# All eleven gate and up blocks as seven products, the first two units interleaved, the first unit's weights split beside the output projection

## The chip, the cores and the metric

The kernel runs on one core of a Trainium2 chip. The metric is the device time of one execution in microseconds (us). One execution was also profiled; its trace gives every instruction's start and duration on the engines: PE is TensorE (matmul), PEld its weight loads, DVE VectorE, ACT ScalarE, POOL GpSimd. SP only issues transfers (DMAs) here.

## What is computed

One layer: three token mixers read a normalised input, their gated sum goes through an output projection and is added to x; then a normalised feed-forward part follows, which is where the change lies. Its sizes: 512 tokens, width 1024, `w_gate` and `w_up` 1024 x 2816, `w_down` 2816 x 1024.

```python
    merged = ...
    x = x + merged @ w_out[layer]

    h2 = rms_norm(x, g_ffn[layer])
    x = x + (jax.nn.silu(h2 @ w_gate[layer]) * (h2 @ w_up[layer])) @ w_down[layer]
```

## The kernel before, in words

**Precision.** Each operand of a matmul is split into a high part (a rounded copy, made by ScalarE) and a low part (what is left, a subtraction on VectorE). A product then takes three passes: high by high, high by low, low by high (`PASSES`).

**Order.** The program is written out by hand: each engine executes its own instructions in the order in which the code emits them, and waits at an instruction until its inputs are there and its output buffer is free. `mm` (L211) emits a matmul and calls `tick` (L196) after each 13 or so of 256 columns; a tick emits half a weight piece's split (`split_next`, L145) and what `later` (L231) has put off for so many ticks. SBUF tiles come from one ring of 47 slots (`slot`, L56), PSUM banks from two rings, three "m" and five "a" (`bank`, L78). SP executes its DMA issues in order too; one that waits holds those behind it.

**Output projection.** `out_group(t, c, W)` (L927) computes token tile t (of four) by 256 columns c (of four): 24 matmuls; VectorE then adds the bank to the residual (tile `x`, L930), ScalarE squares it and sums the squares (`sq`, L932). Columns 0 and 1 are done for all t, then columns 2 and 3 for t = 0, 1, 2, 3 in turn, each followed by `norm2(t)` (L953): the sum of squares, its root (ACT `ra`, `ry`; DVE `rv`, `ra`, `rr`), the normalised row tile `h` (L958), and a DMA of the residual to DRAM (`x_d`, L959), which SP issues when the last `x` of this t is there. After t = 2, `turn2(0)` (L961) transposes the tokens of t = 0 and 1 (16 matmuls against the identity) and evacuates them, split.

**Gate and up.** 2816 columns are eleven blocks of 256. Block 0 is computed plainly: `plain` (L1125, called in the loops below L1132), eight groups of 24 matmuls, with `turn2(1)` after the second group. The other ten blocks are *units*. A unit multiplies a 2 x 2 block matrix of weights by one of activations with seven products instead of eight (M1 to M7, of 24 matmuls each; `product`, L1061), from sums of quarters. `load_unit` (L1005) issues ten DMAs on SP, in this order: S1, S3, A11, A12, A22, each a gate half and an up half of 256 KB (tiles `wq`, L1010), and four adding DMAs on POOL, into S1 and S3. `sums` (L1020) makes S2 and S4 on VectorE (`ws`), `split_op` (L1025) makes the high part `wh` and the low part `wl` of one left operand, 128 x 1024 (L1029, L1030). The right operands are B11, B21, B22 (quarters of the transposed activations) and four sums T1 to T4, split once (`xh`, `xl`). `after` (L1082) evacuates the products, `glu` and its two helpers make silu(gate) x up, split, as tile `gT`. Unit 0 is loaded when the plain block begins; each product carries a list of hooks (`todo`) that are emitted between its matmuls: the evacuation of the product before, the split for the product after next, the loads of the next unit.

**Down.** `down` (L1204) multiplies `gT` by `w_down`, adds the residual and writes out.

Of the kernel before, what the change touches and what calls it, by code (L numbers as in the profile page):

```python
# [42 lines left out]
def hybrid_layer(ctx, tc, rope, x, mem, g_mix, w_in, b_forget, g_q_moba, g_k_moba, g_q_fox,  # L43
# [80 lines left out]
    plan_cols(w_gate, D, DFF, 0, 256)  # L124
    plan_cols(w_up, D, DFF, 0, 256)
# [808 lines left out]
    for c in range(2):  # L934
        W = take(2)
        for t in range(NT):
            out_group(t, c, W)
    W2, W3 = take(2), take(2)
    h2 = {}


    Xf, X = {}, {}
    for kh in range(2):
        for th in range(2):
            Xf[kh, th] = slot("xf")
            X[kh, th] = slot("xh", F32R), slot("xl", F32R)

    def quarter(t):
        return t[:, :1024].rearrange("p (k t) -> p k t", k=4)

    x1_d = dram.tile([NT, P, D], F32, name="x1_d")

    def norm2(t):  # L953
        s1 = sm("s1", 1, 4)
        dve.tensor_reduce(s1, ss2[:, t, :], axis=AX.X, op=OP.add)
        r = rsqrt(s1, 1.0 / D, 1)
        h2[t] = slot("h2")
        dve.tensor_scalar(h2[t][:, :D], x1[t][:, :D], r, None, op0=OP.mult)  # L958
        nc.sync.dma_start(x1_d[t], x1[t][:, :D])  # L959

    def turn2(u):  # L961
        for b4 in range(4):
            tb = bank("a")
            for k2 in range(2):
                k = 2 * b4 + k2
                for t2 in range(2):
                    o = k2 * 256 + t2 * P
                    pe.transpose(tb[:, o:o + P], h2[2 * u + t2][:, k * P:(k + 1) * P], ident)
            for k2 in range(2):
                k = 2 * b4 + k2  # L970
                hi, lo = (quarter(a)[:, k % 4, :] for a in X[k // 4, u])
                evac_split(hi, lo, tb[:, k2 * 256:(k2 + 1) * 256], gcol[:, GFFN + k:GFFN + k + 1])
            c = (2 * b4) % 4 * 256
            pool.tensor_tensor(Xf[b4 // 2, u][:, c:c + 512], f32(X[b4 // 2, u][0][:, c:c + 512]),
                               f32(X[b4 // 2, u][1][:, c:c + 512]), op=OP.add)
# [29 lines left out]
    def load_unit(u):  # L1005
        f0 = 256 * (u + 1)

        def quarter_of(e, t, kh, fh, **how):
            for g, w in enumerate((w_gate, w_up)):
                e.dma_start(  # L1010
                    t[:, g * 512:(g + 1) * 512].rearrange("p (k c) -> p k c", k=4),
                    dsrc(w, kh * 512 * DFF + f0 + fh * P, [[DFF, P], [P * DFF, 4], [1, P]]), **how)

        for name, kh, fh in (("S1", 0, 1), ("S3", 0, 1), ("A11", 0, 0), ("A12", 1, 0), ("A22", 1, 1)):
            t = L[u, name] = slot("wq")
            quarter_of(nc.sync, t, kh, fh)
        quarter_of(nc.gpsimd, L[u, "S1"], 1, 1, accum_op=OP.add)
        quarter_of(nc.gpsimd, L[u, "S3"], 0, 0, accum_op=OP.add)
# [6 lines left out]
    def split_op(u, m):  # L1025

        r = L[u, LEFT[m]]
        hi, lo = slot("wh", F32R), slot("wl", F32R)
        act.activation(full(hi), full(r), AF.Copy)  # L1029
        dve.tensor_tensor(full(lo), full(r), f32(full(hi)), op=OP.subtract)  # L1030
        H[u, m] = full(hi), full(lo)

    def right_sum(name, a, b, op, e):
        t = slot("xt")
        e.tensor_tensor(full(t), full(a), full(b), op=op)
        return t
# [24 lines left out]
    def product(u, m, hooks):  # L1061

        ps = banks[u, m] = bank(TAG[m])
        w = [a.rearrange("p (g k c) -> p g k c", g=2, k=4) for a in H.pop((u, m))]
        r = [quarter(a) for a in B[RIGHT[m]]]
        n = 0
        hooks = deque(hooks)
        for g in range(2):
            for k in range(4):
                for a, b in PASSES:  # L1070
                    pe.matmul(ps[:, g * 256:(g + 1) * 256], w[a][:, g, k, :], r[b][:, k, :],  # L1071
                              start=n % 12 == 0, stop=n % 12 == 11)
# [9 lines left out]
    def after(u, m):  # L1082

        if m == "M1":
# [28 lines left out]
    def glu_end(u, j):  # L1113
# [4 lines left out]
        gT[2 * (u + 1) + j] = (o[:, :512], o[:, 512:1024])  # L1118


    Wg, Wu = take(2), take(2)
    pace["ahead"] = 0
    ps4 = [bank("m"), bank("m"), bank("m"), bank("a")]

    def plain(W, f, ps, th):  # L1125
        for k in range(KD):
            for a, b in PASSES:
                mm(ps[:, th * 256:(th + 1) * 256], W[k // 4][a][:, k % 4, f * P:(f + 1) * P],
                   quarter(X[k // 4, th][b])[:, k % 4, :], 256,
                   (k == 0 and (a, b) == PASSES[0]), (k == KD - 1 and (a, b) == PASSES[-1]))  # L1130

    load_unit(0)  # L1132
    for half in range(2):
        for n, (W, f) in enumerate(((Wg, 0), (Wg, 1), (Wu, 0), (Wu, 1))):
            plain(W, f, ps4[n], half)
            if half == 0 and n == 1:
                turn2(1)
                for j, fn in enumerate(right_t()):
                    later(3 + j, fn)
            if half == 0 and n == 3:  # L1140
                for j, name in enumerate(("S2", "S4")):
                    later(3 + j, lambda name=name: sums(0, name))
                later(5, lambda: split_op(0, "M1"))
                later(6, lambda: split_op(0, "M2"))
    sl = slot("silu")
    for f in range(2):
        act.activation(sl[:, f * 512:(f + 1) * 512], ps4[f], AF.Silu)
    for f in range(2):
        s = sl[:, f * 512:(f + 1) * 512]
        dve.tensor_tensor(s, s, ps4[2 + f], op=OP.mult)  # L1150
        o = slot("gT", F32R)
        evac_split(o[:, :512], o[:, 512:1024], s)
        gT[f] = (o[:, :512], o[:, 512:1024])
    run_due()
    run_pend()
    while deferred:
        run_due()
        run_pend()
# [104 lines left out]
```

## Time and profile before

| | us |
|---|---|
| median of 3 runs (896.21 to 897.88) | 897.0 |
| the profiled execution | 897.43 |
| its span, first to last instruction | 895.6 |
| TensorE busy in it | 875.7 |
| VectorE busy | 566.1 |
| ScalarE busy | 448.8 |
| GpSimd busy | 202.8 |

A row of the timeline has the start in us from the span's start, the duration, engine, line of the kernel, operation, tiles written and read, shape, how many follow each other, and in brackets how long the engine was idle before it and what ended that. A row of a stage table has the stretch, its length, then for each engine the busy time and its instructions, then the granted TensorE clock (1.00 is full speed), the share of time in which the DMA engines were busy, and GB/s. Buffer numbers are left out of names there, so `x1` and `h2` of the code appear as `x` and `h`. A matmul of 256 columns shows about 0.28 us because matmuls overlap; their starts lie some 0.118 us apart.

### The profile page before, as it was taken

Reading aid. Unit: us, or ns where it says so; the run is one execution under the profiler, and the core shown is the slowest. Engines: PE = TensorE matmul, PEld = TensorE weight load, DVE = VectorE, ACT = ScalarE, POOL = GpSimd, SP = SyncE. Lnnn points to the kernel's source line nnn. Section 1 sums busy time; section 2 is a strip of 40 time slices with the busy share of each in tenths; the row PEclk is TensorE's granted clock in tenths of the full one; section 3 lists DMA queues with packets and bytes.
Section 4 is the critical chain, followed back from the end, with each engine's and each line's share of the span. In section 5 each row is a group of like instructions: output and inputs, shape, how many; then the busy total and the mean of one; then the engine's idle time right before and its main releaser. Section 6 shows DMA issues by size and latency. Waiting matters only on the chain.

```text
span 895.6 us, 15494 instructions
## 1 busy us (share of the span) xinstructions
PE 875.7 (98%) x5942; PEld 806.7 (90%) x5942; DVE 566.1 (63%) x1138; ACT 448.8 (50%) x942; POOL 202.8 (23%) x292
## 2 busy tenths in 40 slices
PE   6999999999999999999999999799999999999998
PEld 6999988998899899888888999699999999888886
DVE  4955764666566867787445367888888889842001
ACT  7755764665557557665333444544445445532000
POOL 3222421151212533533000017532222220000000
PEclk9999999999999999999999999799999999999999
DMA  9920332143313512523335019989986886851001
GB/s 309 285 70 25 97 93 71 49 122 92 95 49 112 149 48 70 167 71 119 117 121 186 1 72 196 251 164 179 175 166 120 184 163 144 303 194 48 1 35 59
DMA packets 128361, 111.25 MB, mean 124 GB/s; under 512 B 5072, under 2 KB 119816, under 8 KB 128288
## 3 DMA queue, kind: packets, MB, share of 16 engines
q1 hardware_dynamic: 104320, 93.37, 35.1%
q0 software_dynamic: 22784, 14.78, 11.7%
q10 hardware_dynamic: 1184, 2.12, 0.8%
q8 instruction: 47, 0.77, 0.4%
q14 instruction: 26, 0.21, 0.1%
HBM read 101.85 MB, written 4.21 MB: 118 GB/s over the span
## 4 chain that ended last, share of the span: by engine, by line
PE 86%; DVE 4%; ACT 3%; DMA 2%; POOL 2%; issue 1%; SPq 1%; ACTq 0%; POOLq 0%; DVEq 0%
PE ps_m L215 47%; PE ps_a L1071 13%; PE ps_m L1071 9%; PE ps_a L215 8%; PE ps_a L721 2%; PE ps_a L659 2%; PE ps_a L710 2%; DMA x_t<-in_x_dram 1%; DVE kT L479 1%; PE ps_a L462 1%; DVE w_lo L159 1%; ACT kT L475 1%; DMA wq<-in_w_gate_dram 1%; ACT w_hi L158 1%; PE ps_a L627 0%
## 5 line engine op out<-in xcount | busy, mean ns | idle before, releaser
L159 DVE TENSOR_TENSOR w_lo<-w_raw,w_hi 128x512 fp32r<-128x512 f32 (+1 forms) x212 | 146.0, 721 | 74.5 <-ACT w_hi L158 60.2
L215 PE MATMUL ps_m<-w_hi,hT 128*128 128x256 f32 (+1 forms) x896 | 168.2, 285 | 0.0
L215 PEld LDWEIGHTS ps_m<-w_hi,hT 128*128 128x128 f32 x896 | 139.4, 189 | 0.3
L158 ACT ACTIVATE w_hi<-w_raw 128x512 fp32r<-128x512 f32 (+1 forms) x212 | 123.9, 621 | 28.4 <-PE ps_m L215 19.0
L215 PE MATMUL ps_m<-w_lo,hT 128*128 128x256 f32 (+1 forms) x448 | 127.4, 284 | 0.5 <-DVE w_lo L159 0.5
L215 PE MATMUL ps_m<-hT,w_hi 128*128 128x512 f32 x384 | 123.2, 397 | 0.0
L1071 PE MATMUL ps_a<-xh,wl 128*128 128x256 f32 x320 | 91.2, 285 | 3.9 <-DVE wl L1030 3.9
L1071 PE MATMUL ps_a<-xh,wh 128*128 128x256 f32 x320 | 91.2, 285 | 2.6 <-ACT wh L1029 2.6
L1071 PE MATMUL ps_a<-xl,wh 128*128 128x256 f32 x320 | 91.1, 285 | 0.0
L215 PEld LDWEIGHTS ps_m<-w_lo,hT 128*128 128x128 f32 x448 | 84.5, 189 | 0.9 <-DVE w_lo L159 0.7
L215 PEld LDWEIGHTS ps_m<-hT,w_hi 128*128 128x128 f32 x384 | 71.0, 188 | 14.1
L692 POOL TENSOR_SCALAR p_t<-p_t,rc 128x128 f32<-128x128 f32 (+1 forms) x64 | 40.6, 635 | 171.5 <-DVE rc L691 142.7
L215 PE MATMUL ps_m<-hT,w_lo 128*128 128x512 f32 x192 | 76.5, 398 | 0.0
L215 PE MATMUL ps_a<-w_hi,gT 128*128 128x512 f32 x220 | 71.1, 392 | 0.0
L1071 PE MATMUL ps_m<-xl,wh 128*128 128x256 f32 x240 | 67.5, 281 | 0.0
L1071 PE MATMUL ps_m<-xh,wl 128*128 128x256 f32 x240 | 67.4, 281 | 0.0
L1071 PE MATMUL ps_m<-xh,wh 128*128 128x256 f32 x240 | 67.3, 280 | 0.0
L1071 PEld LDWEIGHTS ps_a<-xh,wl 128*128 128x128 f32 x320 | 61.6, 192 | 4.2 <-DVE wl L1030 4.2
L1071 PEld LDWEIGHTS ps_a<-xh,wh 128*128 128x128 f32 x320 | 61.7, 193 | 2.8 <-ACT wh L1029 2.8
L1030 DVE TENSOR_TENSOR wl<-wq,wh 128x1024 fp32r<-128x1024 f32 x50 | 60.8, 1218 | 2.0 <-ACT wh L1029 2.0
L215 PE MATMUL ps_m<-yT,w_hi 128*128 128x512 f32 x192 | 61.9, 397 | 0.0
L1071 PEld LDWEIGHTS ps_a<-xl,wh 128*128 128x128 f32 x320 | 61.7, 193 | 0.0
(221 smaller groups left out, 1969.0 us busy)
## 6 DMA issues: line engine op xcount, KB each, us to landing
w_raw<-in_w_in_dram SPq DMA_DIRECT2D x50, 512.0 KB, 3.8
wq<-in_w_gate_dram SPq DMA_DIRECT2D x50, 256.0 KB, 5.4
wq<-in_w_up_dram SPq DMA_DIRECT2D x50, 256.0 KB, 6.6
w_raw<-in_w_down_dram SPq DMA_DIRECT2D x22, 512.0 KB, 4.5
wq<-in_w_gate_dram POOLq DMA_DIRECT2D x20, 256.0 KB, 9.3
wq<-in_w_up_dram POOLq DMA_DIRECT2D x20, 256.0 KB, 10.4
w_raw<-in_w_mem_kv_dram SPq DMA_DIRECT2D x8, 512.0 KB, 9.7
kT<-kT POOLq DMA_DIRECT2D x16, 256.0 KB, 4.1
```

Source lines behind the costliest of these rows:

```text
L158: act.activation(hi[:, c], r[:, c], AF.Copy)
L159: pend.append(lambda: dve.tensor_tensor(lo[:, c], r[:, c], f32(hi[:, c]), op=OP.subtract))
L215: pe.matmul(ps, lhsT, rhs, start=start, stop=stop)
L462: pe.transpose(tb[:, tt * P:(tt + 1) * P], raw[:, tt * 256 + blk * P:tt * 256 + (blk + 1) * P], ident)
L475: act.activation(hi[r], tb[r], AF.Copy, scale=g[r])
L479: dve.scalar_tensor_tensor(lo[q if gc in (GQM, GQF) else r], tb[r], g[r], f32(hi[r]), op0=OP.mult, op1=OP.subtract)
L659: pe.matmul(ps[:, :n], Q[p][:, s * 512 + i * P:s * 512 + (i + 1) * P], K[p][s][:, b * 512:b * 512 + n], start=b == 0, stop=b == 1)
L692: pool.tensor_scalar(pt[:, :nk], pt[:, :nk], rc, 1.0, op0=OP.mult, op1=OP.mult)
L710: pe.transpose(tb[:, j * P:(j + 1) * P], pt[:, j * P:(j + 1) * P], ident)
L721: pe.matmul(yb[:, :256], V[p][:, j, 2 * s:2 * s + 2, :], PT[b][:, j, :], start=(j == 0 and b == 0), stop=(j == nj - 1 and b == 1))
L1030: dve.tensor_tensor(full(lo), full(r), f32(full(hi)), op=OP.subtract)
L1071: pe.matmul(ps[:, g * 256:(g + 1) * 256], w[a][:, g, k, :], r[b][:, k, :], start=n % 12 == 0, stop=n % 12 == 11)
```

## The change

The plain block is gone; all eleven blocks are units (`NU` from 10 to 11). Unit 0 is loaded before the output projection, and its seven splits and two sums are emitted at every second tick from column 1 of the projection on. The first two units' products are interleaved (`FIRST`). Units 2 to 10 follow in the old order with the old hooks. `turn2` now takes one quarter (kh, th): it evacuates unsplit (`xf`, alternately by ScalarE and VectorE), and `right_split` splits from there, B11 and B21 in two halves during t = 3, B22 and the sums T1 to T4 within the first products. What GpSimd added before VectorE now does. For units 0 and 1 M3 is evacuated ahead of M5 and M6, by a copy.

```diff
-    plan_cols(w_gate, D, DFF, 0, 256)
-    plan_cols(w_up, D, DFF, 0, 256)
...
+    FIRST = ((0, "M1"), (0, "M2"), (1, "M1"), (1, "M2"), (0, "M3"), (1, "M3"), (0, "M5"), (0, "M6"),
+             (1, "M5"), (1, "M6"), (0, "M7"), (1, "M7"), (0, "M4"), (1, "M4"))
...
+    Ws = take(2)
+    load_unit(0)
+    for c in range(2):
+        if c:
+            Ws = take(2)
+            for j, fn in enumerate((
+                    lambda: split_op(0, "M1"), lambda: sums(0, "S2"), lambda: split_op(0, "M2"),
+                    lambda: sums(0, "S4"), lambda: split_op(0, "M5"), lambda: split_op(0, "M3"),
+                    lambda: split_op(0, "M6"), lambda: split_op(0, "M7"), lambda: split_op(0, "M4"))):
+                later(2 + 2 * j, fn)
+        for t in range(NT):
+            out_group(t, c, Ws)
...
     for t in range(NT):
         out_group(t, 2, W2)
         out_group(t, 3, W3)
         norm2(t)
         if t == 2:
-            turn2(0)
+            for kh, name in ((0, "B11"), (1, "B21")):
+                turn2(kh, 0)
+                right_split(name, Xf[kh, 0], 2)
...
     use_table("silu_and_others")
+    load_unit(1)
...
-    load_unit(0)
-    for half in range(2):
-        for n, (W, f) in enumerate(((Wg, 0), (Wg, 1), (Wu, 0), (Wu, 1))):
-            plain(W, f, ps4[n], half)
...
-    order = [(u, m) for u in range(NU) for m in ORDER]
+    order = list(FIRST) + [(u, m) for u in range(2, NU) for m in ORDER]
...
+    todo[0] += [lambda: split_op(1, "M1")]
+    todo[1] += [lambda: split_op(1, "M2")]
+    todo[2] += [lambda: turn2(1, 1), lambda: turn2(0, 1), lambda: right_split("B22", Xf[1, 1]),
+                lambda: right_sum("T1", Xf[0, 0], Xf[0, 1], OP.subtract),
+                lambda: sums(1, "S2")]
+    todo[3] += [lambda: right_split("T1", T["T1"]), lambda: sums(1, "S4")]
+    todo[4] += [lambda: split_op(1, "M3"),
+                lambda: right_sum("T2", Xf[1, 1], T["T1"], OP.add),
+                lambda: right_split("N2", T["T2"], 1, -1.0)]
```

The products and their left operands are M1: A11, M2: A12, M3: S4, M4: A22, M5: S1, M6: S2, M7: S3.

**VectorE, token tile t = 1 of columns 2 and 3.** Before, from the normalised tile of t = 0 to that of t = 1:

```order
L958 TENSOR_SCALAR h_6382<-x_6008,rr 128x1024
L930 TENSOR_TENSOR x_6010<-ps_m,x_6010 128x256 x2
L955 TENSOR_REDUCE s_6441<-ss_6016 128x1
L267 TENSOR_SCALAR rv<-s_6441 128x1
L275 TENSOR_TENSOR ra<-ry 128x1
L276 SCALAR_TENSOR_TENSOR ra<-ra,rv 128x1
L277 SCALAR_TENSOR_TENSOR rr<-ra,ry 128x1
L958 TENSOR_SCALAR h_6453<-x_6010,rr 128x1024
```

The same place in the changed kernel (its lines are two to 42 off):

```order
L1000 TENSOR_SCALAR h_6385<-x_6008,rr 128x1024
L987 TENSOR_TENSOR wl<-ws,wh 128x1024
L928 TENSOR_TENSOR x_6010<-ps_m,x_6010 128x256
L987 TENSOR_TENSOR wl<-ws,wh 128x1024
L928 TENSOR_TENSOR x_6010<-ps_m,x_6010 128x256
L997 TENSOR_REDUCE s_6452<-ss_6016 128x1
```

One low part of unit 0 now stands ahead of each of the two residual adds; each needs its `wh`, which ScalarE makes behind the square of the `x` above it. The rows from the reduction on are the same.

**SP, from the last weights of the projection to the loads behind it** (`x1_d` is the residual in DRAM, `wq` a quarter of unit weights). Before:

```order
L141 DMA w_raw_6287<-in_w_up_dram 128x4x256
L959 DMA x1_d_6301<-x1_6008 128x1024
L959 DMA x1_d_6301<-x1_6010 128x1024
L959 DMA x1_d_6301<-x1_6012 128x1024
L959 DMA x1_d_6301<-x1_6014 128x1024
L1010 DMA wq_6655<-in_w_gate_dram 128x4x128
L1010 DMA wq_6655<-in_w_up_dram 128x4x128
```

Now:

```order
L963 DMA wq_6030<-in_w_up_dram 128x4x128
L139 DMA w_raw_6072<-in_w_out_dram 128x4x256
L139 DMA w_raw_6110<-in_w_out_dram 128x4x256
L1001 DMA x1_d_6017<-x1_6008 128x1024
L1001 DMA x1_d_6017<-x1_6010 128x1024
L1001 DMA x1_d_6017<-x1_6012 128x1024
L1001 DMA x1_d_6017<-x1_6014 128x1024
L963 DMA wq_6660<-in_w_gate_dram 128x4x128
L963 DMA wq_6660<-in_w_up_dram 128x4x128
L963 DMA wq_6663<-in_w_gate_dram 128x4x128
L963 DMA wq_6663<-in_w_up_dram 128x4x128
L963 DMA wq_6666<-in_w_gate_dram 128x4x128
```

Unit 0's ten loads have moved ahead of the projection's last two pieces; the first loads behind the four residuals are now those of unit 1. `wq_6666` is A11 of unit 1, the operand of the third product.

**ScalarE, from the loading of the silu table on**, where the products begin. Before:

```order
L63 ACT_TABLE_LOAD
L158 ACTIVATE w_hi<-w_raw 128x512 x4
L242 ACTIVATE xh<-ps_a,gcol 128x256 x8
L1040 ACTIVATE xh<-xt 128x1024 x4
L1029 ACTIVATE wh<-wq 128x1024 x2
```

Now:

```order
L63 ACT_TABLE_LOAD
L986 ACTIVATE wh<-wq 128x1024
L1099 ACTIVATE zs<-ps_a 128x512
L986 ACTIVATE wh<-wq 128x1024
L1017 ACTIVATE xf<-ps_a,gcol 128x256 x4
L1025 ACTIVATE xh<-xf 128x1024
L1099 ACTIVATE zs<-ps_a 128x512
L1025 ACTIVATE xh<-xt 128x1024
L986 ACTIVATE wh<-ws 128x1024
```

The high parts of A11 and A12 of unit 1 (the first and second `wh`) now stand ahead of the evacuations `xf` that B22 and T1 to T4 are made from; the last row is the high part of S4 of unit 1.

More of the change, by code (lines that the diff above doesn't have):

```diff
@@ L932, in out_group @@
         act.activation(sq, xs, AF.Square, accum_out=ss2[:, t, c:c + 1])
[L934 to L946, printed above, removed]
+    gT = {}
+    RIGHT = {"M1": "B11", "M2": "B21", "M3": "B22", "M4": "T4", "M5": "T1", "M6": "N2", "M7": "T3"}
@@ L948, in quarter, with full, load_quarters, quarter_of @@
+    def full(t):
+        return t[:, :1024]
     def quarter(t):
         return t[:, :1024].rearrange("p (k t) -> p k t", k=4)
+    PLACE = {"S1": (0, 1), "S3": (0, 1), "A11": (0, 0), "A12": (1, 0), "A22": (1, 1)}
+    def load_quarters(u, names):
+        f0 = 256 * u
+        def quarter_of(e, t, kh, fh, **how):
+            for g, w in enumerate((w_gate, w_up)):
+                e.dma_start(
+                    t[:, g * 512:(g + 1) * 512].rearrange("p (k c) -> p k c", k=4),
+                    dsrc(w, kh * 512 * DFF + f0 + fh * P, [[DFF, P], [P * DFF, 4], [1, P]]), **how)
+        for name in names:
+            t = L[u, name] = slot("wq")
+            quarter_of(nc.sync, t, *PLACE[name])
+        for name, kh, fh in (("S1", 1, 1), ("S3", 0, 0)):
+            if name in names:
+                quarter_of(nc.gpsimd, L[u, name], kh, fh, accum_op=OP.add)
@@ new lines, in load_unit, with sums, split_op @@
+    def load_unit(u):
+        load_quarters(u, ("S1", "S3", "A11", "A12", "A22"))
+    def sums(u, name):
+        a, b = {"S2": ("S1", "A11"), "S4": ("S2", "A12")}[name]
+        t = L[u, name] = slot("ws")
+        dve.tensor_tensor(full(t), full(L[u, a]), full(L[u, b]), op=OP.add)
+    def split_op(u, m):
+        r = L[u, LEFT[m]]
+        hi, lo = slot("wh", F32R), slot("wl", F32R)
+        act.activation(full(hi), full(r), AF.Copy)
+        pend.append(lambda: dve.tensor_tensor(full(lo), full(r), f32(full(hi)), op=OP.subtract))
+        H[u, m] = full(hi), full(lo)
@@ L969, in turn2 @@
             for k2 in range(2):
[L970 to L975, printed above, removed]
+                k = 4 * kh + 2 * b + k2
+                o, i = quarter(x)[:, 2 * b + k2, :], tb[:, k2 * 256:(k2 + 1) * 256]
@@ new lines, in turn2, with right_split @@
+                g = gcol[:, GFFN + k:GFFN + k + 1]
+                if k2 == 0:
+                    act.activation(o, i, AF.Copy, scale=g)
+                else:
+                    dve.tensor_scalar(o, i, g, None, op0=OP.mult)
+    def right_split(name, x, parts=1, sign=1.0):
+        hi, lo = slot("xh", F32R), slot("xl", F32R)
+        w = 1024 // parts
+        for c in (slice(o, o + w) for o in range(0, 1024, w)):
+            act.activation(hi[:, c], x[:, c], AF.Copy, scale=sign)
+            if sign == 1.0:
+                dve.tensor_tensor(lo[:, c], x[:, c], f32(hi[:, c]), op=OP.subtract)
+            else:
+                dve.scalar_tensor_tensor(lo[:, c], x[:, c], sign, f32(hi[:, c]), op0=OP.mult,
+                                         op1=OP.subtract)
+        B[name] = full(hi), full(lo)
@@ L977, in hybrid_layer @@
+    W2, W3 = take(2), take(2)
+    pace["ahead"] = 0
     for t in range(NT):
@@ L1000, in hybrid_layer @@
-    L, H, banks, got, Z = {}, {}, {}, {}, {}
-    def full(t):
-        return t[:, :1024]
[L1005 to L1018, printed above, removed]
@@ L1020, in sums @@
-    def sums(u, name):
-        a, b = {"S2": ("S1", "A11"), "S4": ("S2", "A12")}[name]
-        t = L[u, name] = slot("ws")
-        dve.tensor_tensor(full(t), full(L[u, a]), full(L[u, b]), op=OP.add)
[L1025 to L1036, printed above, removed]
@@ L1061, in product @@
+    while deferred:
+        run_due()
+        run_pend()
+    use_table("silu_and_others")
+    load_unit(1)
     def product(u, m, hooks):
@@ L1082, in after @@
     def after(u, m):
+        early = u < 2
         if m == "M1":
@@ L1117, in glu_end @@
         evac_split(hi, lo, z[:, :, 0, :])
[L1118 to L1130, printed above, removed]
@@ L1132, in hybrid_layer @@
-    load_unit(0)
-    for half in range(2):
-        for n, (W, f) in enumerate(((Wg, 0), (Wg, 1), (Wu, 0), (Wu, 1))):
-            plain(W, f, ps4[n], half)
[L1136 to L1158, printed above, removed]
-    order = [(u, m) for u in range(NU) for m in ORDER]
+        gT[2 * u + j] = (o[:, :512], o[:, 512:1024])
@@ L1170, in hybrid_layer @@
+    todo[8] += [lambda: right_sum("T4", T["T2"], Xf[1, 0], OP.subtract),
+                lambda: right_split("T4", T["T4"])]
+    for n, x in enumerate(order):
+        todo[n + 1].insert(0, lambda x=x: after(*x))
+    for n, (u, m) in enumerate(order):
+        if u > 1 or u == 1 and m not in ("M1", "M2", "M3"):
+            todo[n - 2].append(lambda x=(u, m): split_op(*x))
+    for u in range(2, NU):
+        lead = at[u, "M1"] - (9 if 2 < u < 8 else 7)
         todo[lead].append(lambda u=u: load_unit(u))
-        for name, m in (("S2", "M7"), ("S4", "M4")):
-            todo[at[u - 1, m]].insert(1, lambda u=u, name=name: sums(u, name))
+        for name, n in (("S2", 2), ("S4", 1)):
+            todo[at[u, "M1"] - n].insert(1, lambda u=u, name=name: sums(u, name))
```

68 lines of the change are left out of this document (31 added, 37 removed).

## The prediction

> **What bounds the kernel now.** I read the page, then busy time by stage, then TensorE's waits, its timeline around the one gap, and the chain that ended last.
>
> ```profile
> PE 875.7 (98%) x5942; PEld 806.7 (90%) x5942; DVE 566.1 (63%) x1138; ACT 448.8 (50%) x942; POOL 202.8 (23%) x292
> 537.10:561.50 24.40, 24.40 (x210) 24.36 (x208) 18.79 (x27) 11.77 (x24) 18.89 (x13) 1.00 0.93 199
> 561.60:563.50 1.90, 0.07 (x1) 0.00 (x0) 1.90 (x2) 1.27 (x2) 1.90 (x3) 1.00 0.97 279
> 563.50:569.00 5.50, 0.80 (x2) 0.50 (x2) 5.50 (x6) 2.65 (x4) 3.86 (x3) 0.51 1.25 249
> 569.00:573.80 4.80, 4.79 (x22) 4.79 (x23) 3.41 (x5) 1.72 (x3) 0.00 (x0) 0.50 1.32 213
> 573.80:593.80 20.00, 20.00 (x171) 20.00 (x170) 16.49 (x19) 9.43 (x12) 5.21 (x4) 1.00 0.97 191
> PE ps_a L1071 <- DVE wl L1030: 3.9, 1, 3.9
> PE ps_a L1071 <- ACT wh L1029: 2.6, 1, 2.6
> 537.11 0.28 PE L215 MATMUL ps_m<-xh,w_hi 128*128 128x256 f32 x1
> 561.39 0.28 PE L215 MATMUL ps_a<-xh,w_lo 128*128 128x256 f32 x1
> 569.01 0.58 PE L1071 MATMUL ps_a<-xh,wl 128*128 128x256 f32 x1 [3.93 <-DVE wl L1030]
> 573.85 0.29 PE L1071 MATMUL ps_m<-xh,wh 128*128 128x256 f32 x1
> 574.01 2.83 PE ps_m L1071 x24
> 764.36 5.68 PE ps_a L1071 x48
> 770.05 3.46 PE ps_a L215 x15
> ```
>
> TensorE is busy 98%, so only its gaps and its number of matmuls can be saved. Around the opening there is one gap. The eight plain groups run from 537.11 to 561.5, and the first product, which needs 2.84 us, ends at 573.85. The stage rows (after the sum: PE, PEld, DVE, ACT, POOL, granted clock) show why: it waits for VectorE's `wl`, the clock falls to half near 563.5, and 22 matmuls then run at 0.50 for 4.8 us. That loses 12.35 - 2.84 = **9.5 us**. From 573.85 to 770.05 the other 69 products follow without a gap, 2.843 us each (24 matmuls of 0.1185).
>
> **What the change removes.** The plain block has 192 matmuls, a unit's seven products 168: 24 x 0.1185 = **2.85 us**. The wait in front of the old first product, 9.5 us, goes too, since unit 0's weights are split beside the output projection. Both together are 12.35 us. The 32 transposes stay. GpSimd's sums, the silu block and the loads that served the plain block go too; behind the new waits they cost nothing either way. The remaining nine units keep their hooks.
>
> **What it adds: a longer VectorE queue beside the projection.** Seven splits and two sums of unit 0 now stand between the residual adds `x` and the normalisations. In the blocks t=1 and t=2 each `x` has a `wl` ahead of it, whose ScalarE half stands behind the previous square.
>
> ```profile
> 518.04 0.42 DVE L930 TENSOR_TENSOR x<-ps_m,x 128x256 f32<-128x256 f32 x1
> 520.82 0.42 DVE L930 TENSOR_TENSOR x<-ps_m,x 128x256 f32<-128x256 f32 x1
> 521.34 0.42 ACT L932 ACTIVATE sq<-x 128x256 f32<-128x256 f32 x1 [1.24 <-DVE x L930]
> 523.98 0.75 DVE L930 TENSOR_TENSOR x<-ps_m,x 128x256 f32<-128x256 f32 x2
> 529.88 0.42 DVE L930 TENSOR_TENSOR x<-ps_m,x 128x256 f32<-128x256 f32 x1 [1.99 <-PE ps_m L215]
> 538.66 0.74 DVE L930 TENSOR_TENSOR x<-ps_m,x 128x256 f32<-128x256 f32 x2
> 577.49 1.22 DVE L1030 TENSOR_TENSOR wl<-ws,wh 128x1024 fp32r<-128x1024 f32 x1
> 578.63 1.22 DVE L1030 TENSOR_TENSOR wl<-wq,wh 128x1024 fp32r<-128x1024 f32 x1
> L1029 ACT ACTIVATE wh<-wq 128x1024 fp32r<-128x1024 f32 x50 | 50.1, 1047 | 7.1 <-PE ps_m L1071 3.2 <-PE ps_a L1071 1.9 <-issue 1.6
> 493.64 0.69 DVE L159 TENSOR_TENSOR w_lo<-w_raw,w_hi 128x512 fp32r<-128x512 f32 x1 [1.25 <-ACT w_hi L158]
> 492.98 0.63 ACT L158 ACTIVATE w_hi<-w_raw 128x512 fp32r<-128x512 f32 x1
> ```
>
> From a token tile's last `x` until VectorE is free again takes 523.98 - 520.82 = 3.16 us (square, reduction, root, `h`; it waits in order). A `wl` takes 1.14 from start to start (577.49, 578.63). From an `x` to the `wl` behind it: 0.5 until the square starts, 0.42, `wh` 1.05, a handover, 2.0. So a block takes 3.16 + 1.14 + 2.0 + 1.14 = 7.44 us, while TensorE delivers its two groups in 48 x 0.1185 = 5.7. Block t=0 starts as before (518.04, I take 518.3), so the last `x` of t=0, 1, 2 start at 521.45, 528.9 and 536.35; the last was at 529.88. Then come the 3.16 and the four half splits of B11 and B21: xf pairs of 0.35 a piece, 0.63 and 0.69 per half, in turn between the two engines, 4.6 us, and two `x` (0.74). The residual of t=3 is complete at about **544.85**, was 539.40.
>
> TensorE waits for it twice. The first transposes need `h` of t=1, ready at 528.9 + 3.1 = 532.0 instead of 529.7: **2.3 us**. The first product's second matmul needs the first half of B11's low part at about 541.3; TensorE is there at 539.4: **1.9 us**. M1 and M2 of unit 0 then end at 546.9.
>
> **The wait that decides: unit 1's weights.** SP issues in order, and unit 1's loads stand behind `x_d` of t=3, which waits for that last `x`. The third product, (1,M1), needs A11 of unit 1, the third pair of loads; the fourth needs A12.
>
> ```profile
> 539.43 0.32 SPq L959 DMA_DIRECT2D x_d<-x  x1
> 539.86 0.38 SPq L1010 DMA_DIRECT2D wq<-in_w_gate_dram  x1
> 542.57 0.45 SPq L1010 DMA_DIRECT2D wq<-in_w_gate_dram  x1
> wq<-in_w_gate_dram SPq DMA_DIRECT2D x1, 256.0 KB, 5.3
> 543.80 1.04 SPq L1010 DMA_DIRECT2D wq<-in_w_gate_dram  x1
> wq<-in_w_gate_dram SPq DMA_DIRECT2D x1, 256.0 KB, 6.3
> 544.89 1.29 SPq L1010 DMA_DIRECT2D wq<-in_w_up_dram  x1
> wq<-in_w_up_dram SPq DMA_DIRECT2D x1, 256.0 KB, 8.9
> ```
>
> Each issue row is followed by its landing time from the list of DMA issues. The old unit 0 went through the same queue behind the same `x_d`: first issue 539.86, A11's gate half landed 8.0 later, A12's halves 10.2 and 13.9 later. A11's up half lies between 8.0 and 10.2; I take 9.0. Then it was covered by 24.4 us of plain groups; now the cover is two products, 5.7 us. The new first issue is 544.85 + 0.45 = 545.3, A11 has landed at 554.3, its high part is ready at 555.4, its low part, which the third matmul needs, at 556.65. TensorE came to that matmul at 547.15: **9.5 us**. It is longer than the old gap, so I charge the same half clock, 22 matmuls at 0.213 instead of 0.1185, **2.2 us**.
>
> A12 lands at 545.3 + 13.9 = 559.2, and its `wh` stands on ScalarE ahead of the evacuations that make B22 and T1; its `wl` stands on VectorE ahead of theirs. From there: high and low part 2.25, one addition to z 0.6, two xf 0.7, B22's high part 1.15, so B22's low part starts 4.7 after the landing; five VectorE operations of 1.14 up to the sum S4; its high and low part 2.4. That is 12.9: the third matmul of (1,M3) can go at 572.1. TensorE, with (1,M1), 16 transposes, (1,M2) and (0,M3) behind it, is there at 569.2: **2.9 us**. After that the queues keep up but for about **0.6** at (2,M2), where the opening's backlog on VectorE ends.
>
> Sum: 2.3 + 1.9 + 9.5 + 2.2 + 2.9 + 0.6 = 19.4 us added, 12.35 removed: **+7.1**. The profiled execution took 897.43 (span 895.6), the median is 897.0: I forecast **904.1**.
>
> Bounds: the landing of A11 gives -1.0 to +1.2. The half-split and xf times aren't in the trace; with nothing for xf the chain is 1.4 shorter, at 0.5 each 0.6 longer. The 0.6 may be 0 to 1.5.
>
> The page's clock row speaks on the other two waits. In the trace the clock was full until 563.5, about 1.9 us after the last plain matmul, and half behind it. The Trainium skill, "TensorE: Matmul & The Clock Gate", section "What's actually happening", has the clock fall only after an idle window of about 3.4 us, free-running. By that rule the 2.3 and 2.9 us waits leave it full; here it fell sooner, so I give the case of a second fall its own chance.
>
> **Rivals.**
> - *A second fall of the clock* at the 2.9 us wait: TensorE idles some 2 us, runs two matmuls, idles 0.9. Price 2.2, less the 0.6 that VectorE then catches up: **905.7**. For: the fall after 1.9 us above. Against: waits end here sooner.
> - *Faster loads.* In a later unit A12's up half landed 11 after the first issue (616.62 to 627.6):
>
> ```profile
> 616.62 0.37 SPq L1010 DMA_DIRECT2D wq<-in_w_gate_dram  x1
> 620.51 1.58 SPq L1010 DMA_DIRECT2D wq<-in_w_up_dram  x1
> wq<-in_w_up_dram SPq DMA_DIRECT2D x1, 256.0 KB, 7.1
> ```
>
>   With it A11 comes some 1.5 earlier; behind it the 16 transposes at half clock then hold B22, so little more is gained: **902**. The Trainium skill, "DMA: Bandwidth & Descriptors", section "Anatomy of one DMA — SWDGE (gpsimd) path", fits a transfer (there one issued by GpSimd) by 2.0 us and its bytes at 436 GB/s; for the 2.4 MB up to A12 that estimate is 7.4 us after the first issue, and the sum would be near 899. The trace's 13.9 stands against it.
> - *Faster:* unit 1's loads aren't held, because SP gets past `x_d` early or the VectorE lag is absent. Then 9.5, 2.2 and 2.9 fall away and 4.2 to 4.8 stay: 897.0 - 12.35 + 4.5 = **889**. It decides where the loads start some 7 us earlier, at about 538, before even the old `x_d`. Against: the old first load followed `x_d` by 0.4 us.
> - *No change:* two thirds of VectorE's lag (5.45 us at `x_d`) don't come, and the loads are fast as above: 7.1 - 3.6 - 2 = 1.5, **898.5**.
>
> **How the numbers follow.** Forecast 0.52, second fall 0.20, faster loads 0.14, no change 0.06, faster 0.08. The range, 899.5 to 908.0, takes the first three with their bounds and leaves out the last two. A measurement of this kernel tells some 0.2% (1.8 us) from no change: faster 0.08, same 0.06, slower 0.86.
>
> **What would show it.** In the profile after: residual adds of t=2 near 536 with a `wl` before each; a TensorE gap of 2 us at the first transposes; a gap of 8 to 11 us ended by `wh` and `wl` of L986 and L987 in the third product, half clock behind it; SP's load of unit 1 starting right behind the last `x_d`, near 545; a wait of 2 to 4 us in the sixth product. It would be wrong if the third product waits less than 5 us, or if the first loads of unit 1 start before 541.

## The result, and the profile after

The changed kernel takes **906.6 us** (median of 4 runs, 906.2 to 907.9); the kernel before, timed beside it, takes 897.3. The ratio is 1.0108, with a 95% interval of 1.009 to 1.0125: slower by about 1%. The profiled execution took 906.42, with a span of 904.7 (before: 897.43 and 895.6). The forecast was 904.1, with a range of 899.5 to 908.0. Of all executions below one, of experiment 1, ran in a slow state of the chip (1064.57 us at a mean granted clock of 0.755), and it is left out.

First the page of the changed kernel, busy time by engine:

```profile
PE 877.7 (97%) x5918; PEld 807.5 (89%) x5918; DVE 571.5 (63%) x1145; ACT 452.9 (50%) x941; POOL 191.3 (21%) x286
```

There are 24 matmuls fewer (5942 before), and yet TensorE is busy 2 us longer. Matmuls that run at half clock count as busy, so the next view has to be read with the column of the granted clock. Busy time by stage (the columns are those of the same view of before: the stretch, its length, then PE, PEld, DVE, ACT, POOL, the granted clock, the DMA share and GB/s):

```profile
528.00:541.00 13.00, 9.68 (x79) 9.05 (x78) 8.74 (x23) 6.84 (x18) 0.00 (x0) 1.00 0.21 82
546.00:562.00 16.00, 7.12 (x34) 6.62 (x33) 5.13 (x8) 4.99 (x8) 5.16 (x4) 0.68 1.20 234
568.00:576.00 8.00, 5.85 (x34) 5.44 (x33) 6.36 (x7) 2.61 (x4) 5.19 (x4) 0.79 1.15 269
576.00:778.95 202.95, 202.85 (x1705) 202.64 (x1704) 175.96 (x208) 99.73 (x125) 41.66 (x32) 1.00 0.83 173
...
555.96:561.63 5.67, 5.67 (x27) 5.67 (x27) 2.68 (x5) 2.48 (x4) 0.00 (x0) 0.50 1.32 200
571.87:575.28 3.41, 3.41 (x18) 3.41 (x17) 2.29 (x3) 1.54 (x2) 2.63 (x3) 0.50 1.27 256
```

A stretch less its instructions at 0.1185 each is what it lost. (A row also counts the two that reach across its edges; 77, 32, 32 and 1703 start inside.) That is 13.00 - 9.12 = **3.9**, 16.00 - 3.79 = **12.2**, 8.00 - 3.79 = **4.2** and 202.95 - 201.8 = **1.1**: 21.4 us. The change removes 12.35, so +9.05 is left, and the span grew by 9.1: the account closes to 0.1 us. TensorE's waits put a name to it:

```profile
PE ps_a L1081 <- ACT wh L986: 8.4, 1, 8.4
PE ps_a L1011 <- DVE h L1000: 2.1, 1, 2.1
PE ps_m L1081 <- ACT wh L986: 1.4, 1, 1.4
PE ps_a L1081 <- ACT xh L1025: 0.9, 1, 0.9
PE ps_m L1081 <- DVE wl L987: 0.8, 1, 0.8
PE ps_a L1081 <- DVE wl L987: 0.5, 1, 0.5
PE ps_a L1081 <- DVE xl L1027: 0.3, 1, 0.3
```

Each happens once: 2.1 at the first transposes, 0.9 + 0.3 in the first product, **8.4 + 0.5 in the third product, (1,M1), that is M1 of unit 1**, and 1.4 + 0.8 in (1,M3). The timeline shows where the 8.4 come from (start, duration, engine, line, operation; in brackets the idle time ahead and what ended it):

```profile
526.99 1.23 DVE L987 TENSOR_TENSOR wl<-ws,wh 128x1024 fp32r<-128x1024 f32 x1 [1.52 <-ACT wh L986]
528.13 0.42 DVE L928 TENSOR_TENSOR x<-ps_m,x 128x256 f32<-128x256 f32 x1
...
534.30 1.23 DVE L987 TENSOR_TENSOR wl<-wq,wh 128x1024 fp32r<-128x1024 f32 x1 [1.52 <-ACT wh L986]
535.44 0.42 DVE L928 TENSOR_TENSOR x<-ps_m,x 128x256 f32<-128x256 f32 x1
...
543.31 0.75 DVE L928 TENSOR_TENSOR x<-ps_m,x 128x256 f32<-128x256 f32 x2
544.09 0.32 SPq L1001 DMA_DIRECT2D x_d<-x  x1
544.50 0.39 SPq L963 DMA_DIRECT2D wq<-in_w_gate_dram  x1
...
553.59 1.06 ACT L986 ACTIVATE wh<-wq 128x1024 fp32r<-128x1024 f32 x1 [6.77 <-DMA wq<-in_w_up_dram]
557.39 1.06 ACT L986 ACTIVATE wh<-wq 128x1024 fp32r<-128x1024 f32 x1 [2.27 <-DMA wq<-in_w_up_dram]
569.19 1.06 ACT L986 ACTIVATE wh<-ws 128x1024 fp32r<-128x1024 f32 x1 [2.43 <-DVE ws L980]
570.28 1.22 DVE L987 TENSOR_TENSOR wl<-ws,wh 128x1024 fp32r<-128x1024 f32 x1 [0.52 <-ACT wh L986]
```

Read it from top to bottom. The last residual adds of t=1 and t=2 stand at 528.13 and 535.44 with a `wl` ahead of each. SP's store `x_d` of t=3 follows the last add at 544.09, and the first load of unit 1 follows the store 0.4 us later. ScalarE's `wh` of A11 starts at 553.59, the moment the load lands, 9.1 after its queue began; that of A12 at 557.39, 12.9 after. `wh` and `wl` of S4, which (1,M3) waits for, come at 569.19 and 570.28.

### The profile page after: what moved, and what is told of

Its sections match the earlier page's. It is cut to its first block, busy times and chain, and to the rows that moved or that the text cites. A ratio compares the mean times of both kernels' runs of the same rounds, so it can differ in the third digit from the quotient of the medians.

```text
span 904.7 us, 15456 instructions
## 1 busy us (share of the span) xinstructions
PE 877.7 (97%) x5918; PEld 807.5 (89%) x5918; DVE 571.5 (63%) x1145; ACT 452.9 (50%) x941; POOL 191.3 (21%) x286
## 4 chain that ended last, share of the span: by engine, by line
PE 81%; DVE 8%; ACT 5%; issue 2%; DMA 1%; POOL 1%; SPq 0%; ACTq 0%; DVEq 0%; POOLq 0%
PE ps_m L213 43%; PE ps_a L1081 12%; PE ps_m L1081 9%; PE ps_a L213 8%; PE ps_a L719 2%; PE ps_a L657 2%; PE ps_a L708 2%; DVE wl L987 2%; DVE w_lo L157 1%; ACT w_hi L156 1%; ACT wh L986 1%; DVE kT L477 1%; PE ps_a L460 1%; DVE ws L980 1%; DMA wq<-in_w_up_dram 1%
## 5 line engine op out<-in xcount | busy, mean ns | idle before, releaser
L1081 PE MATMUL ps_a<-xh,wh 128*128 128x256 f32 x352 | 100.1, 285 | 9.3 <-ACT wh L986 8.4
L1081 PE MATMUL ps_a<-xh,wl 128*128 128x256 f32 x352 | 100.1, 284 | 0.5 <-DVE wl L987 0.5
L1081 PE MATMUL ps_a<-xl,wh 128*128 128x256 f32 x352 | 99.8, 284 | 0.3 <-DVE xl L1027 0.3
L963 POOL DMA_DIRECT2D wq<-in_w_gate_dram x22 | 31.5, 1431 | 267.2 <-DMA wq<-in_w_gate_dram 126.8
L987 DVE TENSOR_TENSOR wl<-wq,wh 128x1024 fp32r<-128x1024 f32 x55 | 67.0, 1218 | 17.3 <-ACT wh L986 17.3
L1081 PE MATMUL ps_m<-xh,wh 128*128 128x256 f32 x264 | 75.2, 285 | 1.4 <-ACT wh L986 1.4
L1081 PE MATMUL ps_m<-xh,wl 128*128 128x256 f32 x264 | 75.2, 285 | 0.9 <-DVE wl L987 0.8
L1081 PEld LDWEIGHTS ps_a<-xh,wh 128*128 128x128 f32 x352 | 67.2, 191 | 9.7 <-ACT wh L986 8.6
L1081 PE MATMUL ps_m<-xl,wh 128*128 128x256 f32 x264 | 75.0, 284 | 0.0
L1081 PEld LDWEIGHTS ps_a<-xh,wl 128*128 128x128 f32 x352 | 67.1, 191 | 0.8 <-DVE wl L987 0.8
```

What stands on the lines that cost most here:

```text
L963: e.dma_start(t[:, g * 512:(g + 1) * 512].rearrange("p (k c) -> p k c", k=4), dsrc(w, kh * 512 * DFF + f0 + fh * P, [[DFF, P], [P * DFF, 4 ...
L987: pend.append(lambda: dve.tensor_tensor(full(lo), full(r), f32(full(hi)), op=OP.subtract))
```

## The experiments

All edits are against the changed kernel. The base case for the expectations is its 906.6.

### 1. The store behind the loads

```diff
+        if t < 3:
             nc.sync.dma_start(x1_d[t], x1[t][:, :D])
...
     load_unit(1)
+    nc.sync.dma_start(x1_d[3], x1[3][:, :D])
```

> Only SP's order is changed: the store x_d of t=3 stands behind the ten loads of unit 1 instead of ahead of them. Theory (the loads are late because SP holds them behind that store, which waits for VectorE): the first load is issued near 536.3, right behind x_d of t=2 (535.9 in the changed kernel), A11 has landed 9.0 later at 545.3, and the third product's wait of 8.4 + 0.5 and the half clock behind it (10.2 us long, about 3.1 lost) go. A12 (549.2) then no longer sets the start of (1,M3); what sets it is the chain from the second transposes over B22, T1, S2, S4 (8.2 from the start of B22's low part to the end of S4's), which ends near 562 while TensorE is there at 558: a wait of about 4 in place of 2.2, with a fall of the clock behind it. Sum 906.6 - 8.9 - 3.1 + 1.8 + 0.5 = about 897. Rival A (the transfers themselves are what is late, because other traffic holds them): A11 lands as late as before, 906.6. Rival B (nothing replaces the wait): 906.6 - 8.9 - 3.1 - 2.2 - 1.5 = 891.

Measured: 897.57 (median of nine executions, 895.71 to 899.86), ratio to the kernel before 0.9999 (0.9988 to 1.001). The profiled execution is the slowest of the nine. Its timeline, SP's issues and ScalarE around A11:

```profile
536.29 0.32 SPq L1002 DMA_DIRECT2D x_d<-x  x1
536.70 0.39 SPq L963 DMA_DIRECT2D wq<-in_w_gate_dram  x1
...
545.94 1.28 ACT L63 ACT_TABLE_LOAD   x1
547.23 1.06 ACT L986 ACTIVATE wh<-wq 128x1024 fp32r<-128x1024 f32 x1
549.32 1.06 ACT L986 ACTIVATE wh<-wq 128x1024 fp32r<-128x1024 f32 x1 [0.54 <-DMA wq<-in_w_up_dram]
```

The one edit moves the loads from 544.50 to 536.70, and some 9 us of time go. Rival A is out: the transfers were late because they were issued late. Rival B is out too: the loads are not all that waits. A11's `wh` no longer waits for its DMA (nothing in brackets) but stands behind the loading of the silu table, and TensorE still waits 1.6 + 0.8 there and 1.2 + 0.8 at (1,M3). The latter is less than the 4 us expected.

### 2. Unit 0's splits one column group earlier

```diff
         if c:
             Ws = take(2)
+        else:
             for j, fn in enumerate((
```

> Unit 0's seven splits and two sums are started one column group earlier, so that none stands in the blocks of column groups 2 and 3. Theory (the `wl` ahead of each `x` makes the blocks 7.4 us instead of TensorE's 5.7): the last `x` of t=1 and t=2 move from 528.1 and 535.4 to about 524.7 and 530, the waits of 2.1 at the first transposes and 0.9 + 0.3 in the first product go, x_d of t=3 is issued near 539.5 instead of 544.1 and the third product still waits 8 (its loads start 4.5 earlier and TensorE comes 3.5 earlier): 906.6 - 3.5 - 1.0 = about 902. Rival (the lag comes from the chain square, reduction, root, h itself and not from the splits): residual adds as before, 906.6.

Measured: 906.08, ratio 1.0092 (1.0077 to 1.0107). The four `x_d`, each behind the last residual add of its tile, were issued at 526.5, 530.5, 536.2 and 544.4: the blocks of t=1 and t=2 took 4.0 and 5.7, where those of the changed kernel took 7.3. So the splits do lengthen the blocks. But the waits show that the time was only moved:

```profile
PE ps_a L1082 <- ACT wh L986: 6.2, 1, 6.2
PE ps_m L213 <- ACT w_hi L156: 4.2, 1, 4.2
```

The splits now hold up those of the projection's own weights, and TensorE stops for 4.2, until 519.25, at the start of column groups 2 and 3. The store of t=3, and so unit 1's loads, stay where they were. The expectation of 902 missed that. As a test of the lag the run settles only half; experiment 5 is the cleaner one. (The profiled execution, 904.07, is the fastest of the four; the others took 905.9 to 906.4.)

### 3. A11 and A12 first in the queue

```diff
-        load_quarters(u, ("S1", "S3", "A11", "A12", "A22"))
+        load_quarters(u, ("A11", "A12", "S1", "S3", "A22") if u == 1 else ("S1", "S3", "A11", "A12", "A22"))
```

> Unit 1's loads in the order A11, A12, S1, S3, A22 instead of S1, S3, A11, A12, A22; their start stays where it is (544.5). Theory (a load's landing is set by its place in the queue behind the late start): A11 has landed 4.6 after the first issue instead of 9.0, the wait in the third product falls from 8.9 to about 4.5. S1 and its accumulation come some 4 us later (563), the chain S2, S4 hangs on them, and (1,M3) still waits some 2.8. 906.6 - 4.4 + 0.6 = 902.8 if the clock falls as before, about 900 if a wait of 4.5 leaves it full. Rival (all ten loads share the bandwidth and land together, whatever their order): A11 at +8 to +9, 906.

Measured: 901.27, ratio 1.0047 (1.0032 to 1.0062). In the profiled execution (903.18, the slowest of four) the loads still begin at 545.53, behind `x_d`, but ScalarE has A11 4.7 later:

```profile
550.27 1.06 ACT L986 ACTIVATE wh<-wq 128x1024 fp32r<-128x1024 f32 x1 [2.41 <-DMA wq<-in_w_up_dram]
```

The wait in the third product fell to 4.1 + 0.8. The clock fell behind it all the same, for 6.8 us instead of 10.2. A load's landing goes by its place in the queue; the bandwidth is not shared evenly among the ten. S1's later accumulation cost nothing that shows: (1,M3) waited 1.2 + 0.8.

### 4. The gap filled with matmuls

```diff
         n = 0
+        if (u, m) == (1, "M1"):
+            for _ in range(66):
+                pe.matmul(ps[:, :256], r[0][:, 0, :128], r[0][:, 1, :], start=True, stop=True)
```

> 66 matmuls whose result is overwritten (7.8 us) are put ahead of the third product, into its own bank, so that TensorE is busy during most of the wait for A11; nothing else changes. Theory (the half clock follows from the idle time): no half clock at 551 to 561. The 3.1 us that it cost in place come back only in part, because (1,M3) then waits for the chain behind A12 (landed 557.3, chain of about 12.9): third matmul of (1,M3) at about 570.2 instead of 572.3, its wait 3.5 to 4 instead of 2.2. 905.0 if the clock falls at that wait again, 903.5 if it doesn't. Rival A (the clock falls for another reason than TensorE's idle time, or the half clock costs nothing): 906.6. Rival B (the full 3.1 come back, the chain is held by the transposes alone): 903.5 with a second fall as now, 902 without it.

Measured: 907.76, ratio 1.0119 (1.0097 to 1.0142). In the profiled execution the half clock behind the third product shrank from 10.2 us to 3.4, but nothing was gained. A12 came later:

```profile
556.45 1.06 ACT L986 ACTIVATE wh<-wq 128x1024 fp32r<-128x1024 f32 x1 [8.46 <-DMA wq<-in_w_up_dram]
562.25 1.06 ACT L986 ACTIVATE wh<-wq 128x1024 fp32r<-128x1024 f32 x1 [4.25 <-DMA wq<-in_w_up_dram]
```

From the first issue (545.66) A11 took 10.8 and A12 16.6; without the fill they took 9.1 and 12.9. From A12's `wh` to (1,M3)'s third matmul (575.32) it took 13.1, in the changed kernel 14.2. That fits the chain behind A12 setting that point, with about one microsecond added by the transposes at half clock. Whether the matmuls slowed the transfers or this was chance was not tried; the runs spread from 906.0 to 910.8. The profiled execution is the slowest of them, and in it the half clock lasted as long in all as in the changed kernel, 13.65 us: 3.41 at the first transposes, 3.41 here and 6.83 at (1,M3), against 10.24 and 3.41. The other three executions had a mean clock of 0.998, which leaves some 4 us of half clock, and still took 906.0 to 908.3. So less half clock did not by itself make the kernel faster; what those three waited for instead is not on record.

### 5. The low part two ticks behind the high part

```diff
-        pend.append(lambda: dve.tensor_tensor(full(lo), full(r), f32(full(hi)), op=OP.subtract))
+        low = lambda: dve.tensor_tensor(full(lo), full(r), f32(full(hi)), op=OP.subtract)
+        if u == 0:
+            later(2, low)
+        else:
+            pend.append(low)
```

> In unit 0's splits the VectorE half (`wl`) is issued two ticks behind its ScalarE half (`wh`) instead of right behind it, so that VectorE doesn't stand in front of an unfinished `wh`; the work is the same and all else stays. Theory (half of the lag is VectorE waiting in order for ScalarE, 1.5 to 1.6 in front of each `wl`): the blocks of t=1 and t=2 take 5.8 instead of 7.3, the last `x` of t=1 and t=2 come near 526.3 and 532.1 (were 528.1 and 535.4), the wait at the first transposes (2.1) and that in the first product (1.2) go, x_d of t=3 is issued near 542 (was 544.1). TensorE comes 3.3 earlier to the third product and its loads 2 to 2.5, so the third product waits about 10. Sum about 904. Rival (VectorE's sum of work, not its order, makes the lag): 906.6, x_d at 544.

Measured: **900.55**, ratio 1.0036 (1.0023 to 1.0049). VectorE's timeline in this run:

```profile
525.02 0.42 DVE L928 TENSOR_TENSOR x<-ps_m,x 128x256 f32<-128x256 f32 x1
525.35 1.21 DVE L987 TENSOR_TENSOR wl<-ws,wh 128x1024 fp32r<-128x1024 f32 x1
526.48 0.42 DVE L928 TENSOR_TENSOR x<-ps_m,x 128x256 f32<-128x256 f32 x1
...
532.19 0.42 DVE L928 TENSOR_TENSOR x<-ps_m,x 128x256 f32<-128x256 f32 x1
...
541.20 0.75 DVE L928 TENSOR_TENSOR x<-ps_m,x 128x256 f32<-128x256 f32 x2
```

No `wl` has a wait ahead of it any more, the block of t=2 takes 5.7 (532.19 - 526.48), and the store of t=3 goes at 541.98. The waits at the transposes and in the first product are gone; the third product waits 9.4 + 0.5, as expected. The time fell by 6 us, 3.5 more than I had worked out. In the profiled execution (900.55) two things differ that I had left as they were: the clock did not fall at (1,M3), which had cost 2.0, and behind the third product the half clock ended 4.2 us after TensorE resumed (552.5 to 556.7), where it had taken 6.9 (554.7 to 561.6); half of the difference, 1.3, is time won. Together that is 3.3, and that the clock fell less was not planned.

### 6 to 8. Towards a faster kernel

Experiment 6 puts 1 and 5 together and takes the silu table out of A11's way:

```diff
-    use_table("silu_and_others")
     load_unit(1)
...
+    todo[5] += [lambda: use_table("silu_and_others")]
```

> Three moves at once: x_d of t=3 behind unit 1's loads (as in the first experiment), `wl` two ticks behind `wh` (as in the one before), and the loading of the silu table from ahead of the products to the sixth, so that it no longer stands on ScalarE ahead of A11's `wh`. Theory (VectorE's chain B22, T1, S2, S4 sets the start of (1,M3) once the loads are early): third product waits about 2.6, (1,M3) about 4.5, and the clock falls once or twice for 1.7 each: 896. Rival (with early loads and a shorter lag nothing waits any more): 887 to 889.

Measured: 894.27, ratio 0.9959 (0.9945 to 0.9974), with 1.3 + 1.1 in the third product, 1.4 + 0.8 in (1,M3) and a fall of the clock at each. What the table's move is worth by itself was not measured. Experiment 7 adds a new order of VectorE's queue:

```diff
-    todo[1] += [lambda: split_op(1, "M2")]
+    todo[1] += [lambda: split_op(1, "M2"), lambda: sums(1, "S2"), lambda: sums(1, "S4")]
...
-                lambda: right_sum("T1", Xf[0, 0], Xf[0, 1], OP.subtract),
-                lambda: sums(1, "S2")]
-    todo[3] += [lambda: right_split("T1", T["T1"]), lambda: sums(1, "S4")]
-    todo[4] += [lambda: split_op(1, "M3"),
-                lambda: right_sum("T2", Xf[1, 1], T["T1"], OP.add),
+                lambda: right_sum("T1", Xf[0, 0], Xf[0, 1], OP.subtract)]
+    todo[3] += [lambda: split_op(1, "M3"), lambda: right_split("T1", T["T1"])]
+    todo[4] += [lambda: right_sum("T2", Xf[1, 1], T["T1"], OP.add),
```

> The kernel of the run before, and the sums S2 and S4 of unit 1 stand ahead of B22 and T1 in VectorE's order, the split of S4 right behind B22. Theory (it is the order of VectorE's queue that delays S4): the wait of (1,M3) falls from about 4.5 to 1 or less, the third product's 2.6 stay: 891 (889 to 893). Rival (S1's accumulation or A12 land too late for it, or the work is only pushed on to B22 and (0,M3)): 895 to 897, with the wait at (0,M3) or (1,M3).

Measured: **890.06**, ratio 0.9917 (0.9903 to 0.9932): faster than both kernels. VectorE's timeline of it:

```profile
546.53 1.22 DVE L987 TENSOR_TENSOR wl<-wq,wh 128x1024 fp32r<-128x1024 f32 x1 [1.28 <-ACT wh L986]
547.67 1.22 DVE L980 TENSOR_TENSOR ws<-wq 128x1024 f32<-128x1024 f32 x1
548.92 1.23 DVE L980 TENSOR_TENSOR ws<-ws,wq 128x1024 f32<-128x1024 f32 x1
...
554.94 1.22 DVE L987 TENSOR_TENSOR wl<-ws,wh 128x1024 fp32r<-128x1024 f32 x1
```

S2 and S4 are done before B22 is there, and S4's low part ends at 556.2. (1,M3) waits no longer; 1.3 + 1.1 in the third product are left. Experiment 8 went for those by putting the loads and A11's split ahead of the normalisation of t=3:

```diff
+        if t == 3:
+            load_unit(1)
+            split_op(1, "M1")
+            run_pend()
         norm2(t)
...
-    todo[0] += [lambda: split_op(1, "M1")]
```

> The kernel of the run before, and the loads of unit 1 and the split of its A11 stand ahead of the normalisation of t=3. Theory (what is left of the third product's wait is VectorE's normalisation ahead of `wl`): its wait falls by 1 to 1.5, 890 (888 to 892). Rival (A11's landing is what ends it): as the run before, or up to 1.5 slower since the normalisation, and with it the second transposes, waits behind A11.

Measured: 890.73, ratio 0.9923 (0.9908 to 0.9937). The rival was right: 1.1 us went from the third product, and 1.0 came at the second transposes, which now wait for the normalisation, and 0.9 behind them at B22's low part.

### 9 and 10. The clock

```diff
         n = 0
+        if (u, m) == (1, "M3"):
+            for _ in range(8):
+                pe.matmul(ps[:, :256], r[0][:, 0, :128], r[0][:, 1, :], start=True, stop=True)
```

> The changed kernel with 8 matmuls (0.95 us, their result is overwritten) ahead of (1,M3), which has waited there for 1.40 and, two matmuls later, for 0.76. They stand inside the first wait, so nothing is put off. Theory (the clock is looked at in stretches of 3.41 us that run on by themselves, and falls behind a stretch in which TensorE was idle for more than about 1.7): the stretch 568.45 to 571.87 had 2.15 idle; with the fill some 1.2, the clock stays full, and about 1.7 to 2 of half clock go: 904.9. Rival A (any wait over 1 us brings the fall, or it has another cause): falls as before, 906.6. Rival B (no fall, but VectorE's backlog behind it takes the gain up): 906.

Measured: 905.0, ratio 1.0078 (1.0066 to 1.0091), where the changed kernel had 1.0108 (1.009 to 1.0125). Stretches of 3.41 us in this run:

```profile
528.29:531.70 3.41, 1.30 (x12) 1.07 (x11) 2.19 (x9) 1.86 (x5) 0.00 (x0) 1.00 0.39 154
531.70:535.11 3.41, 3.41 (x17) 3.41 (x18) 1.89 (x3) 1.46 (x3) 0.00 (x0) 0.50 0.02 5
569.25:572.66 3.41, 2.32 (x17) 2.11 (x18) 2.36 (x2) 0.98 (x2) 3.41 (x4) 1.00 1.09 287
```

At (1,M3) TensorE was busy 2.32 of 3.41 and the clock stayed full. At the first transposes, which nobody had touched, it was busy 1.30 and the clock fell behind it; in the profiled execution of the changed kernel it hadn't. So the half clock lasted 13.65 us in all in both (3.41 and 10.24 here), and the gain hangs on where it lay: at the first transposes it cost little, since the wait of 0.9 + 0.3 in the first product is gone in this run and unit 1's first load is issued at 544.77, against 544.50. The two intervals just touch, but the five executions (904.6 to 905.9) all lie below the four of the changed kernel (906.2 to 907.9). Experiment 10 has the same fill, ahead of (1,M1), in the kernel of experiment 7:

> The fastest kernel so far (sums first, 890.1) with 8 such matmuls ahead of (1,M1), where TensorE waited 1.28 and 1.05 and the clock fell behind a stretch with 1.93 idle. By the same theory idle falls to about 1.2 and the half clock of 3.41 us (some 1.7 to 1.9 lost) goes: 888.3. Rivals as there: 890.1 with a fall as before, or 889.5 with the gain taken up by the later waits (0.53, 0.45, 0.39).

Measured: 889.59, ratio 0.9909 (0.9893 to 0.9924). The clock is full throughout the opening, but the 0.5 us can't be told from the kernel without the fill. The larger gain expected, 1.8, did not come.

## Why the prediction was right, step by step

The mechanism was the forecast's, with one of its rivals, the second fall of the clock, on top of it; the range held the time, and the sum was 2 us short (+7.1 forecast, +9.05 accounted for above).

- **The lag of VectorE.** Forecast: last `x` of t=1 and t=2 at 528.9 and 536.35, blocks of 7.44. Measured: 528.13 and 535.44, blocks of 7.3. Its two waits were put at 2.3 and 1.9; they were 2.1 and 1.2, and the stretch 528 to 541 lost 3.9 against 4.2. Experiment 5 shows how much of the lag is VectorE standing in front of an unfinished `wh`: the store of t=3 went at 539.43 before, 544.09 now and 541.98 there, so 2.1 of 4.7. The rest, the work itself, was not taken apart.
- **Loads held on SP behind `x_d`.** Forecast: first issue at 545.3, measured 544.50. Experiment 1 changes nothing but this order and takes some 9 us back. The rival "faster" needed loads that start near 538; its price of 889 was too good, since with the loads that early (536.70) experiment 1 still took 897.57; experiments 6 and 7, which move the table and VectorE's work too, came to 894.27 and 890.06.
- **The wait in the third product.** 9.5 forecast, 8.9 measured; A11 landed 9.1 after the first issue, as taken from the old unit 0. The rival "faster loads" needed A11 some 1.5 earlier, and it did not come; A12 took 12.9, between the rival's 11 and the forecast's 13.9.
- **The half clock behind it.** This term was too small: 2.2 forecast for 22 matmuls of one product. The stretch 546 to 562 lost 12.2, less the wait 3.3, because the half clock lasted until 561.63 and took in the second transposes too, which stand between the matmuls of this product.
- **(1,M3).** 2.9 forecast, 1.4 + 0.8 measured. Its rival, a second fall of the clock, had a chance of 0.20, and it came: 571.87 to 575.28 at 0.50, so the stretch 568 to 576 lost 4.2. A fall after 1.9 us of idling had been seen in the trace of before; the forecast gave it too little weight. Experiment 9 took this fall away and got 905.0, with a fall at the first transposes in its place that cost little.
- **VectorE's backlog.** 0.6 forecast; the stretch from 576 to 778.95 lost 1.1: some 0.4 between 596 and 616, with the one step of 0.38 from matmul to matmul at 601.58, and the rest spread over the whole stretch. What makes the rest is open.
- **Removed: 12.35.** The 24 matmuls are gone (5942 to 5918), and the account closes to 0.1 us with this number.

So the terms are 2.0 short together. The half clock is 3.1 above its forecast (3.3 and 2.0 against 2.2), the waits are 2.2 below theirs (14.4 against 16.6), and small losses behind waits and later make up 1.1. That the sum came within 2.0 is in part luck, since the error of the half clock and that of the waits have opposite signs. In the working, 22 matmuls at 0.213 instead of 0.1185 make 2.1 and not 2.2, the chain behind A12 adds up to 12.8 and not 12.9, and the eight loads up to A12 are 2.1 MB and not 2.4; none of this moves the forecast by more than 0.1.

## What to carry to other kernels

A load that shares an in-order queue with a store is as late as the last engine that the store waits for: when work is taken away from between a load and its first use, look at what stands ahead of the load in its queue, and put the stores behind it. Splitting off work "beside" a busy engine is free only if the engine that takes it doesn't stand waiting in order: here the same `wl`, issued two ticks later, gave back 6 us, some 3 of them through a clock that happened to fall less. Where a wait is only a few microseconds long, count it against the clock's stretches too; its price can double, as at (1,M3) from 2.2 to 4.2. But see first what TensorE would wait for next at full clock: in experiment 4 three executions had little half clock left and were no faster.

## What the runs showed of the clock

Within an execution the clock changed only at edges that lie 3.41 us, or a multiple of it, apart. In the twelve profiled executions (before, changed, ten experiments) I compared TensorE's idle time in each such stretch at full clock with the clock behind it. Busy time in three stretches of the changed kernel (the first number behind the length is TensorE's):

```profile
544.56:547.97 3.41, 1.72 (x15) 1.51 (x13) 1.54 (x6) 1.80 (x5) 0.00 (x0) 1.00 0.91 271
547.97:551.39 3.42, 0.00 (x0) 0.00 (x0) 0.00 (x0) 0.00 (x0) 2.57 (x2) 1.00 1.09 284
568.45:571.87 3.42, 1.27 (x8) 0.86 (x8) 2.90 (x4) 1.06 (x1) 2.56 (x2) 1.00 0.99 280
```

The same view of experiment 1:

```profile
545.55:548.97 3.42, 1.66 (x12) 1.25 (x11) 1.88 (x5) 3.16 (x5) 0.50 (x1) 1.00 1.28 237
```

And of experiment 7:

```profile
541.49:544.90 3.41, 1.48 (x11) 1.06 (x9) 2.33 (x7) 2.24 (x7) 0.27 (x1) 1.00 1.31 225
```

With 1.72 busy (idle 1.69) the clock stayed full; with 1.66, 1.48 and 1.27 busy (idle 1.75, 1.93, 2.15) it was half in the next stretch. Of the stretches at full clock that have a whole stretch behind them, all 19 with 1.75 or more idle were followed by a fall, and none of the 17 with 1.0 to 1.69 idle: the line lies at about half of the 3.41. The same wait of 2.1 us at the first transposes cost a fall where it lay within one stretch (experiments 1 and 9) and none where an edge cut it into 1.66 and 0.45 (the changed kernel). So the edges, whose place differs from execution to execution, decide over some 2 us. In the nine executions of experiment 1 the three with a mean clock of 1.00 took 895.7 to 896.3, the six at 0.992 to 0.996 took 897.3 to 899.9. The Trainium skill, "TensorE: Matmul & The Clock Gate", section "What's actually happening", has free-running windows of about 3.4 us, and these runs agree; it has the clock fall after an idle window, and here half an idle window was enough.
